# Second mixer's attention with the values stationary and the turned probabilities moving; GpSimd normalises before the turning

## Chip, cores and metric

One core of a Trainium2 chip runs one program: a hybrid layer (neighbourhood attention beside a state-space scan, then a gated feed-forward), and behind it a layer of windowed attention with its own feed-forward. The metric is the device time in microseconds. The kernel before takes 1371.63 us, the median of three runs (1370.94 to 1371.93).

## What is computed

The change lies in the mixer of the second layer: 512 tokens in four blocks of 128, 16 query heads over 4 key and value heads of 64 features. A block sees itself and its two neighbours, and each head has one sink logit that takes a part of the softmax and carries no value.

```python
def windowed_gqa_sink(h, w_qkv, w_o, sink, rel_bias):
    q, k, v = split(h @ w_qkv)                  # 1024, 256 and 256 columns
    scores = einsum('bnqhgd,bnkhd->bnhgqk', q, k_band) * (dh ** -0.5)
    logits = where(mask, scores + bias, -1e30)  # k_band: blocks n-1, n, n+1
    p = softmax(concatenate([logits, sink_l], -1), -1)[..., :-1]
    out = einsum('bnhgqk,bnkhd->bnqhgd', p, v_band)
    return out.reshape(B, S, ATT_Q_HEADS * dh) @ w_o
```

So a head has four blocks of queries, with 2, 3, 3 and 2 blocks of keys: ten blocks of 128 by 128 probabilities.

## The kernel before

**Numbers in two parts.** Products are taken to nearly full precision: a float32 operand is split into a high part that is rounded to the faster type fp32r and a low part, the rest; ScalarE writes the high part (a copy), VectorE the low one (a subtraction). A projection is then three matmuls (`mm3`, L88 to L91: high by high, low by high, high by low). A matmul whose operands are plain float32 is not split by the kernel; it appears in the profile as two weight loads and two matmuls.

**Stages.** First layer's mixer, its feed-forward, the second layer's attention (about 815 to 1000 us of the profile), and its feed-forward. `wide` (L943) makes a projection 128 columns at a time: for each such tile the weights come by DMA from a fixed list (`load_w`, L134: ScalarE L151, VectorE L152), 24 matmuls of 512 columns fill a bank of PSUM (L89 to L91), and `use` takes it from there. Attention is hung on `use` (`use_and_attend`, L1094): after two tiles of keys and one of queries the values are made (L1099 to L1109), and from then on each further tile of queries is followed by two heads; the last two heads follow the last tile.

**A head** (`head`, L1044). For each of the four query blocks: two matmuls make the scores (L1059, L1060; 256 or 384 columns); VectorE adds the bias and finds the row's maximum in one instruction (L1062); ScalarE takes the exponential and its sum (L1064); TensorE turns the 2 or 3 blocks (`tr`, L1067; a transpose is a matmul with the identity); ScalarE or VectorE in turn copies the turned blocks to SBUF (L1072, L1070); and for each block the turned probabilities are loaded as weights while the 64 value columns move (L1075, plain float32, ten per head, 320 matmuls in the profile for 16 heads). Then the sum with the sink is formed and inverted (L1076 to L1078), and one VectorE instruction scales the result by it into the natural layout `on` (L1079). After heads 13 and 15, `turn_o` (L1084) turns one half of `on` each (heads 0 to 7, heads 8 to 15) back to features by tokens (L1088, 32 transposes in all) and splits it (L1090, L1091) for the output projection `att_w_o` (`nat_out`, L826; its matmuls are L836).

**What sets the order.** The code above is written head after head, but a scheduler of the framework lays out each engine's instructions when the program is built, with estimates of its own; it mixes the matmuls of the next query tile between the steps of the heads. On the chip each engine then runs its list strictly in that order. Buffers are rings: three banks for scores, two for turned blocks, one for the heads' output, two for projections.

Of the kernel before, what the change touches and what calls it, by code (L numbers as in the profile page):

```python
# [38 lines left out]
def tile_hybrid_then_windowed_gqa(ctx, tc, A, out, dbg=None):  # L39
# [15 lines left out]
    def H():  # L55
        """h^T in two parts, 8 blocks of features each, tokens along"""
        return [hp_.tile([128, 8, S], F32R, tag=t, name=nm(t)) for t in ("hh", "hl")]
# [8 lines left out]
    def psum(**roles):  # L66
        """the eight banks, shared out anew"""
        for r, ids in roles.items():
            ring = itertools.cycle(ids)
            pst[r] = lambda ring=ring: banks[next(ring)]()  # L70
# [31 lines left out]
    def chunks():  # L102
        """every piece of a weight, in the order of its use: tensor, row block, row blocks, columns"""
# [30 lines left out]
    def load_w(src, k0, nk, pieces, room=None):  # L134
        """the next piece of the plan as two fp32r parts, in halves of a row if room is given;
        the pieces after it are on their way"""
# [34 lines left out]
    # ada_w columns of the first shift and scale, 128 features each at a time  # L171
# [45 lines left out]
    def gemv(src, c0, ci):  # L217
        """partial sums, over the partitions, of vec @ src[:, c0:c0 + 1024]; in steps, the last gives the sums"""
# [35 lines left out]
    def mod_job(o, src, c_sh, c_sc, ci, b_sh, b_sc, w, bank):  # L254
        """o: columns of shift, and of norm weight * (1 + scale); in steps, which leave the engines free between"""
# [6 lines left out]
    def gate_job(g, src, c0, ci, rb, rw, bank):  # L262
        """g: gate as a row on all partitions, times a norm weight if there is one; in steps"""
# [27 lines left out]
    # vec @ ada_w for c and c_ctx at once: rows c hi, c_ctx hi, c lo, c_ctx lo, which pick2 then adds  # L291
# [55 lines left out]
    def features(rows, j, v, hi, lo, n):  # L347
        """features 128 j.. of the modulated rows, features on partitions"""
# [49 lines left out]
    def wide_tile(W, c0, hh, hl, n=S, w=None):  # L398
        """PSUM tile [W columns c0..c0 + 127, n tokens]"""
# [34 lines left out]
    # rows 0..15 hi @ h, rows 16..31 lo @ hi of h; pick16 adds the two  # L434
# [12 lines left out]
    p = PT()  # L447
# [67 lines left out]
    # cum[i] - cum[j] on [j, (head of four, i)] is a product: left [group; -cum[j] of the group], right [cum[i]; 1]; cum in two parts  # L515
# [303 lines left out]
    def tick(n):  # L819
        """n steps of about a microsecond went to the tensor engine: what was put off till then"""  # L820
# [5 lines left out]
    def nat_out(src, lhs, evac, ks, after=None, room=None, roomy=2):  # L826
        """[tokens, 1024] = lhs @ src over row blocks ks; the last few go a token block at a time,
        roomy of them with their weights in tiles of room"""
# [54 lines left out]
    def to_hT(mod, row=None):  # L883
        """h^T and what fills it with a token block; with a row, of the norm with that weight, which settle leaves in x"""
# [58 lines left out]
    def wide(W, hh, hl, cols, use):  # L943
        """tiles of (W column block)^T h^T; the first four run a half of the tokens at a time"""
# [67 lines left out]
    PP = slots(ap_, "pp", 3)  # L1012

# [7 lines left out]
    on = [ap_.tile([128, 4, 512], F32, tag=f"on{a}", name=f"on{a}") for a in range(2)]  # L1021
# [20 lines left out]
    po2 = []  # L1042

    def head(h):  # L1044
        kvh = h // 4
        bt = BI(n=384)
        nc.sync.dma_start(out=bt, in_=A["bias2"][h])
        if h % 2 == 0:
            po2.append(PO())
# [223 lines left out]
```

## Time and profile before

| what | value |
|---|---|
| median of three runs | 1371.63 us |
| span of the profiled execution (the page gives no other time of it) | 1369.5 us |
| busy, whole span | TensorE 97%, VectorE 58%, ScalarE 44%, GpSimd 7% |
| granted TensorE clock, mean | 0.991 of full speed |
| stretch 835 to 960 us | the heads: TensorE 124.2 us busy of 125, GpSimd idle |

How to read it: the span runs from the first to the last instruction; a timed run also holds what lies around it. PE is TensorE's matmuls, PEld its weight loads, DVE VectorE, ACT ScalarE, POOL GpSimd. Matmuls are pipelined, so the duration of one (some 270 ns for a small one) is longer than the distance from one start to the next; what a matmul costs the engine is read from starts, or from the chain of waits, which gives each stretch of time to one instruction only.

### The profile page before, as it was taken

How to read it: one execution, taken by the hardware profiler on the slowest of the kernel's cores; microseconds unless marked ns; L12 is line 12 of the kernel's file. 1: busy time of each engine (PE TensorE's matmuls, PEld its weight loads, DVE VectorE, ACT ScalarE, POOL GpSimd, SP SyncE). 2: the span in 40 equal slices, each digit the busy share in tenths (PEclk: the TensorE clock that was granted, in tenths of full speed). 3: DMA queues.
4: the chain of work that ended last, by engine and by line, in shares of the span. 5: the costliest groups of instructions: out<-in, count | busy, mean ns of one | idle time of the engine just before them, and what ended most of it. 6: DMA issues, size and time to landing. Idle time of an engine off the chain costs nothing. (4 is left out here: it accounts for less than half of the span.)

```text
span 1369.5 us, 18243 instructions
## 1 busy us (share of the span) xinstructions
PE 1332.8 (97%) x6943; PEld 1108.9 (81%) x6943; DVE 793.5 (58%) x1432; ACT 599.5 (44%) x1076; POOL 95.5 (7%) x101
## 2 busy tenths in 40 slices
PE   7999999999999999999999989999999999999997
PEld 3688778887879888888888789888888888888886
DVE  4887985447567747765963566666463222225323
ACT  4656446654626333333432456656462222224321
POOL 0012650000000000000000220000000000000000
PEclk9999999999999999999999999999999999999999
DMA  9955111025192637764764303211223333332221
GB/s 287 266 183 153 34 54 51 24 84 182 34 312 86 186 104 232 232 199 138 245 220 135 93 16 101 76 61 43 78 78 94 106 93 93 102 98 93 95 90 62
DMA packets 176631, 168.15 MB, mean 123 GB/s; under 512 B 7584, under 2 KB 153120, under 8 KB 176544
## 3 DMA queue, kind: packets, MB, share of 16 engines
q1 hardware_dynamic: 176544, 166.99, 38.9%
q8 instruction: 55, 0.90, 0.3%
q14 instruction: 32, 0.26, 0.1%
HBM read 164.87 MB, written 2.10 MB: 122 GB/s over the span
## 5 line engine op out<-in xcount | busy, mean ns | idle before, releaser
L90 PE MATMUL bank<-hl,wh 128*128 128x512 f32 (+1 forms) x1040 | 388.4, 373 | 1.3 <-DVE hl L928 0.7
L91 PE MATMUL bank<-hh,wl 128*128 128x512 f32 (+1 forms) x1040 | 388.1, 373 | 0.0
L89 PE MATMUL bank<-hh,wh 128*128 128x512 f32 (+1 forms) x1040 | 387.9, 375 | 0.0
L151 ACT ACTIVATE wh<-wr 128x1024 fp32r<-128x1024 f32 x173 | 182.4, 1059 | 413.1 <-PE bank L90 302.0
L152 DVE TENSOR_TENSOR wl<-wr,wh 128x1024 fp32r<-128x1024 f32 x173 | 213.8, 1237 | 204.1 <-ACT wh L151 204.0
L90 PEld LDWEIGHTS bank<-hl,wh 128*128 128x128 f32 x1040 | 196.7, 189 | 32.3 <-DVE hl L928 1.7
L89 PEld LDWEIGHTS bank<-hh,wh 128*128 128x128 f32 x1040 | 196.2, 189 | 32.7 <-DVE hh L927 0.6
L91 PEld LDWEIGHTS bank<-hh,wl 128*128 128x128 f32 x1040 | 196.8, 189 | 31.8
L836 PE MATMUL bank<-wh,act 128*128 128x512 f32 x544 | 146.2, 389 | 0.0
L836 PEld LDWEIGHTS bank<-wh,act 128*128 128x128 f32 x544 | 102.1, 188 | 21.5 <-issue 0.2
L226 DVE SCALAR_TENSOR_TENSOR acc<-ada,cs,acc 128x1024 f32<-128x1024 f32 x70 | 91.5, 1308 | 16.0 <-DMA ada<-in_ada_w 15.4
L836 PE MATMUL bank<-wl,act 128*128 128x512 f32 x272 | 84.1, 389 | 0.0
L983 DVE TENSOR_TENSOR act<-bank,act 128x512 f32<-128x512 f32 x44 | 30.4, 690 | 89.7 <-PE bank L91 89.6
L207 POOL TENSOR_TENSOR sm<-sm,mh 128x1 f32<-128x1 f32 x28 | 18.3, 654 | 660.3 <-DVE sm L206 660.3
L836 PEld LDWEIGHTS bank<-wl,act 128*128 128x128 f32 x272 | 51.0, 188 | 10.6
L836 PE MATMUL bank<-act,act 128*128 128x512 f32 x240 | 55.2, 390 | 0.0
L836 PEld LDWEIGHTS bank<-act,act 128*128 128x128 f32 x240 | 44.9, 188 | 9.2
L1075 PEld LDWEIGHTS bank<-v,pp 128*128 128x128 f32 x320 | 41.3, 191 | 5.5 <-ACT pp L1072 2.3
L1075 PE MATMUL bank<-v,pp 128*128 128x64 f32 x320 | 43.1, 271 | 0.1
L993 DVE TENSOR_TENSOR act<-act,act 128x512 fp32r<-128x512 f32 x44 | 29.4, 686 | 21.9 <-PE bank L836 21.9
L1064 ACT ACTIVATE sc<-sc,ss 128x256 f32<-128x256 f32 (+1 forms) x64 | 35.6, 557 | 12.7 <-DVE ss L1062 8.8
L1062 DVE CUSTOM_DVE_ANT_0 sc<-bank,bi,nsink 128x256 f32<-128x256 f32 (+1 forms) x64 | 33.6, 542 | 10.1 <-PE bank L1060 8.2
(333 smaller groups left out, 1946.6 us busy)
## 6 DMA issues: line engine op xcount, KB each, us to landing
ada<-in_ada_w SPq DMA_DIRECT2D x80, 512.0 KB, 4.9
wr<-in_ffn_w_up SPq DMA_DIRECT2D x44, 512.0 KB, 4.5
wr<-in_ffn_w_in SPq DMA_DIRECT2D x44, 512.0 KB, 3.7
wr<-in_w_in SPq DMA_DIRECT2D x23, 512.0 KB, 3.9
wr<-in_ffn_w_down SPq DMA_DIRECT2D x22, 512.0 KB, 4.3
wr<-in_ffn_w_out SPq DMA_DIRECT2D x22, 512.0 KB, 3.5
wr<-in_att_w_qkv SPq DMA_DIRECT2D x12, 512.0 KB, 3.9
ada<-in_ada_w SPq DMA_DIRECT2D x16, 256.0 KB, 4.8
```

Of the source, the lines that this page charges most:

```text
L89: mm(o, lh, rh, start=start, stop=False)
L90: mm(o, lh, rl, start=False, stop=False)
L91: mm(o, ll, rh, start=False, stop=stop)
L151: act(hi[:, :n], raw[:, :n], AF.Copy)
L152: V.tensor_sub(lo[:, :n], raw[:, :n], hi[:, :n])
L226: V.scalar_tensor_tensor(acc, raw, csil[:, ci + k:ci + k + 1], acc, op0=ALU.mult, op1=ALU.add)
L836: mm(ps[tb][a], l, r[a], start=start and l is lh and r is w[0], stop=stop and l is ll)
L983: V.tensor_mul(actT[ft], p, actT[ft])
L993: V.tensor_sub(lo, actT[k], hi)
L1062: V.tensor_tensor_reduce(sc[:, :w], s[:, :w], bt[:, b0:b0 + w], -1.0, nsink[:, h:h + 1], ALU.add, ALU.min, st[:, n:n + 1])
L1064: act(sc[:, :w], sc[:, :w], AF.Exp, scale=-1.0, bias=st[:, n:n + 1], accum_out=st[:, 4 + n:5 + n])
L1075: mm(o, P[:, 128 * i:128 * i + 128], vv[j0 + i][:, 64 * kvh:64 * kvh + 64], start=i == 0, stop=i == nk - 1)
```

## The change

The head is cut in two. The four softmaxes come first and leave four blocks of exponentials in seven buffers (`sc_ring`: four of the ring `xn`, three of `sc`); then the sum with the sink is formed and inverted. In the second half GpSimd multiplies each block of exponentials by the row's inverse sum (L1072 of the changed kernel), TensorE turns them as before (L1075), ScalarE writes the high part of the turned probabilities (L1079) and VectorE the low part (L1080) into two tiles `ph` and `pl`, one of each for the whole kernel, laid out by key block. The values stand in two parts side by side, 64 columns high and 64 low, and are loaded as the 128 weight columns; for each of the four key blocks the 256 or 384 turned columns that see it move past them, first high, then low (L1086: eight matmuls a head, all in fp32r). The result has features on partitions: the products with the high values in one half of the partitions, with the low values in the other. ScalarE copies one half across (L1092), VectorE adds the other (L1093), and after each second head the pair is split once (L1096, L1097) and is ready as one row block of the output projection. `turn_o`, the copies L1070 and L1072 and the scaling L1079 of the kernel before are gone.

```diff
-    PP = slots(ap_, "pp", 3)
+    sc_ring = itertools.cycle([XN] * 4 + [PS_] * 3)
...
-            sc = PS_(n=384)
+            sc = next(sc_ring)(n=384)
             V.tensor_tensor_reduce(sc[:, :w], s[:, :w], bt[:, b0:b0 + w], -1.0, nsink[:, h:h + 1],
                                    ALU.add, ALU.min, st[:, n:n + 1])
             act(sc[:, :w], sc[:, :w], AF.Exp, scale=-1.0, bias=st[:, n:n + 1], accum_out=st[:, 4 + n:5 + n])
+            scs.append(sc)
+        act(st[:, 8:12], st[:, 0:4], AF.Exp, bias=sk[:, h:h + 1])
+        V.tensor_add(st[:, 12:16], st[:, 4:8], st[:, 8:12])
+        V.reciprocal(st[:, 16:20], st[:, 12:16])
+
+        ph, pl = (ap_.tile([128, 4, 512], F32R, tag=f"on{a}", name=nm("p")).rearrange("p a b -> p (a b)")
+                  for a in range(2))
+        for n, (j0, j1) in enumerate(spans):
+            nk, sc = j1 - j0, scs[n]
+            GP.tensor_scalar(sc[:, :128 * nk], sc[:, :128 * nk], st[:, 16 + n:17 + n], None, op0=ALU.mult)
             pt = PT()
             for i in range(nk):
                 tr(pt[:, 128 * i:128 * i + 128], sc[:, 128 * i:128 * i + 128], ident)
-            P = PP(n=384)
-            if n % 2:
-                V.tensor_copy(P[:, :w], pt[:, :w])
-            else:
-                act(P[:, :w], pt[:, :w], AF.Copy)
-            o = po[:, 64 * n:64 * n + 64]
-            for i in range(nk):
-                mm(o, P[:, 128 * i:128 * i + 128], vv[j0 + i][:, 64 * kvh:64 * kvh + 64], start=i == 0, stop=i == nk - 1)
...
-        V.tensor_tensor(on[h // 8][:, :, 64 * (h % 8):64 * (h % 8) + 64], hd(po, 4),
-                        st[:, 16:20, None].to_broadcast([128, 4, 64]), op=ALU.mult)
+            at = 256 * j0 + 128 * n + 128
+            hi, lo = (t[:, at:at + 256 * nk].rearrange("p (k n) -> p k n", k=nk)[:, :, 0:128] for t in (ph, pl))
+            src = pt[:, :128 * nk].rearrange("p (k n) -> p k n", k=nk)
+            act(hi, src, AF.Copy)
+            V.tensor_sub(lo, src, hi)
+        po = PO()
+        for j in range(4):
+            n0, n1 = max(0, j - 1), min(4, j + 2)
+            a = 384 * j + 128 * (n0 - j + 1)
+            for part in (ph, pl):
+                mm(po[:, 128 * n0:128 * n1], vv[j][:, 128 * kvh:128 * kvh + 128], part[:, a:a + 128 * (n1 - n0)],
+                   start=j == 0 and part is ph, stop=j == 3 and part is pl, skip_group_check=True)
+        own, other = slice(64 * (h % 2), 64 * (h % 2) + 64), slice(64 - 64 * (h % 2), 128 - 64 * (h % 2))
+        if h % 2 == 0:
+            op.append(TM())
+        o = op[-1]
+        act(o[own, :], po[other, :], AF.Copy)
+        V.tensor_add(o[own, :], po[own, :], o[own, :])
+        if h % 2:
+            hi, lo = Q(F32R), Q(F32R)
+            act(hi, o, AF.Copy)
+            V.tensor_sub(lo, o, hi)
+            oT[h // 2] = hi, lo
...
-    def turn_o(a):
-        for tb in range(4):
-            p = PT()
-            for f in range(4):
-                tr(p[:, 128 * f:128 * f + 128], on[a][:, tb, 128 * f:128 * f + 128], ident)
-            hi, lo = Q(F32R), Q(F32R)
-            act(hi, p, AF.Copy)
-            V.tensor_sub(lo, p, hi)
-            oT[tb, a] = hi, lo
...
-                t = VV()
-                V.tensor_copy(t, pv)
-                vv.extend([t[:, 0:256], t[:, 256:512]])
+                t = VV(F32R, 1024)
+                tv = t.rearrange("p (g s d) -> p g s d", g=8, s=2)
+                act(tv[:, :, 0, :], hd(pv, 8), AF.Copy)
+                V.tensor_sub(tv[:, :, 1, :], hd(pv, 8), tv[:, :, 0, :])
+                vv.extend([t[:, 0:512], t[:, 512:1024]])
...
-        hi, lo = oT[tb, k // 4]
-        c = slice(128 * (k % 4), 128 * (k % 4) + 128)
+        hi, lo = oT[k]
+        c = slice(128 * tb, 128 * tb + 128)
         return hi[:, c], lo[:, c]
```

The scheduler lays the new program out anew. Two places show how the instructions stand (L numbers of the kernel concerned; a number behind a name tells one use of a buffer from another).

TensorE, head 6 before, from its second score block to its third turned block: `bank_7779` is the head's output, L1067 the turning, L1075 the product with the values, L89 to L91 the next query tile.

```order
L1067 MATMUL bank_7800<-id_102,sc_7797 128x128 x3
L89 MATMUL bank_7910<-hh_6599,wh_7906 128x512
L1059 MATMUL bank_7872<-q_7065,q_7610 128x384
L1060 MATMUL bank_7872<-q_7068,q_7610 128x384
L90 MATMUL bank_7910<-hl_6600,wh_7906 128x512
L91 MATMUL bank_7910<-hh_6599,wl_7907 128x512
L1075 MATMUL bank_7779<-v_7232,pp_7790 128x64 x2
L1067 MATMUL bank_7815<-id_102,sc_7812 128x128 x3
```

TensorE, head 6 now: `bank_7883` is the head's output, L1075 the turning, L1086 the product with the values (`p_7855` high, `p_7856` low), L1057 the next pair's scores.

```order
L1075 MATMUL bank_7858<-id_102,xn_7831 128x128 x2
L1075 MATMUL bank_7864<-id_102,sc_7837 128x128 x3
L90 MATMUL bank_7974<-hl_6600,wh_7970 128x512
L91 MATMUL bank_7974<-hh_6599,wl_7971 128x512
L89 MATMUL bank_7974<-hh_6599,wh_7970 128x512
L1086 MATMUL bank_7883<-p_7855,v_7230 128x256
L90 MATMUL bank_7974<-hl_6600,wh_7970 128x512
L91 MATMUL bank_7974<-hh_6599,wl_7971 128x512
L1075 MATMUL bank_7871<-id_102,sc_7843 128x128 x3
L89 MATMUL bank_7974<-hh_6599,wh_7970 128x512
L1075 MATMUL bank_7878<-id_102,sc_7849 128x128 x2
L1086 MATMUL bank_7883<-p_7856,v_7230 128x256
```

Before, a product followed its own block's turning and copying; now the first product waits for two blocks, the other seven for all or nearly all, and three matmuls of the query tile stand between.

ScalarE, the same pair before: L1064 the exponentials, L1072 the copies of turned blocks, L1076 the sink, L1037 a query tile.

```order
L1064 ACTIVATE sc_7812,ss_7780<-sc_7812,ss_7780 128x384
L1037 ACTIVATE q_7774<-bank_7746 64x512
L1072 ACTIVATE pp_7790<-bank_7787 128x256
L1064 ACTIVATE sc_7827,ss_7780<-sc_7827,ss_7780 128x256
L1076 ACTIVATE ss_7780<-ss_7780,misc_806 128x4
L1072 ACTIVATE pp_7819<-bank_7815 128x384
```

ScalarE, the end of head 6 now: L1079 the high parts of head 6 (`p_7855`), L1062 and L1064 the exponentials and the sink of head 7, L1096 the split of the pair 4 and 5, L1036 a query tile, L1092 the copy across of head 6.

```order
L1079 ACTIVATE p_7855<-bank_7858 128x2x128
L1079 ACTIVATE p_7855<-bank_7864 128x3x128
L1096 ACTIVATE q_7784<-tm_7712 128x512
L1062 ACTIVATE xn_7913,ss_7897<-xn_7913,ss_7897 128x384
L1036 ACTIVATE q_7819<-bank_7794 64x512
L1079 ACTIVATE p_7855<-bank_7871 128x3x128
L1079 ACTIVATE p_7855<-bank_7878 128x2x128
L1062 ACTIVATE xn_7919,ss_7897<-xn_7919,ss_7897 128x256
L1036 ACTIVATE q_7822<-bank_7794 64x512
L1064 ACTIVATE ss_7897<-ss_7897,misc_806 128x4
L151 ACTIVATE wh_8676<-wr_8328 128x1024
L1092 ACTIVATE tm_7892<-bank_7883 64x512
```

All four turned blocks now pass through ScalarE, where two of four did; between the last high part and the copy across stand other work of the neighbouring heads and a weight tile.

## Rows read from the trace of the kernel before

**Rows 1.** The page: span and busy time, whole program.

```profile
span 1369.5 us, 18243 instructions
PE 1332.8 (97%) x6943; PEld 1108.9 (81%) x6943; DVE 793.5 (58%) x1432; ACT 599.5 (44%) x1076; POOL 95.5 (7%) x101
```

**Rows 2.** Busy us by stretch (length, PE, PEld, DVE, ACT, POOL, clock, DMA): heads; four pairs.

```profile
835.00:960.00 125.00, 124.19 (x849) 108.61 (x849) 82.89 (x241) 78.16 (x209) 0.00 (x0) 1.00 0.20 61
...
sum 58.00, PE 58.00 PEld 50.98 DVE 38.60 ACT 36.22 POOL 0.00; mean PE 14.50 PEld 12.75 DVE 9.65 ACT 9.06 POOL 0.00
```

**Rows 3.** Instructions in time, ScalarE: the same copy in two query tiles that follow.

```profile
883.21 0.57 ACT L1037 ACTIVATE q<-bank 64x512 fp32r<-64x512 f32 x1
...
898.03 0.58 ACT L1037 ACTIVATE q<-bank 64x512 fp32r<-64x512 f32 x1
```

**Rows 4.** The chain of waits, 850 to 925 us, shares by line.

```profile
by line: PE bank L1075 30.1%; PE bank L1067 15.1%; PE bank L90 13.1%; PE bank L91 12.7%; PE bank L89 12.3%; PE bank L1059 9.2%; PE bank L1060 7.8%
```

**Rows 5.** Instructions in time, TensorE: start and length of runs.

```profile
903.13 1.45 PE L1075 MATMUL bank<-v,pp 128*128 128x64 f32 x12
904.41 0.39 PE L1067 MATMUL bank<-id,sc 128*128 128x128 f32 x2
```

**Rows 6.** Groups by form, 835 to 960 us, ScalarE.

```profile
L1064 ACT ACTIVATE sc<-sc,ss 128x384 f32<-128x384 f32 x32 | 19.5, 610 | 2.4 <-DVE ss L1062 2.4
...
L1072 ACT ACTIVATE pp<-bank 128x384 f32<-128x384 f32 x16 | 7.9, 492 | 4.2 <-PE bank L1067 3.9
L1037 ACT ACTIVATE q<-bank 64x512 fp32r<-64x512 f32 x12 | 7.0, 584 | 0.1
L1072 ACT ACTIVATE pp<-bank 128x256 f32<-128x256 f32 x16 | 6.1, 384 | 4.2 <-PE bank L1067 4.1
L1090 ACT ACTIVATE q<-bank 128x512 fp32r<-128x512 f32 x8 | 4.7, 596 | 5.3 <-PE bank L1088 5.3
```

**Rows 7.** Groups by form, 850 to 925 us, VectorE.

```profile
L1038 DVE SCALAR_TENSOR_TENSOR q<-bank,q 64x512 fp32r<-64x512 f32 x10 | 6.9, 688 | 0.3
L152 DVE TENSOR_TENSOR wl<-wr,wh 128x1024 fp32r<-128x1024 f32 x5 | 6.1, 1220 | 0.0
L1070 DVE COPY pp<-bank 128x384 f32<-128x384 f32 x10 | 5.6, 558 | 0.2
L1070 DVE COPY pp<-bank 128x256 f32<-128x256 f32 x11 | 4.7, 425 | 13.7 <-ACT ss L1076 9.5 <-PE bank L1067 4.1
L1079 DVE TENSOR_TENSOR on<-bank,ss 128x256 f32<-128x256 f32 x10 | 4.2, 425 | 4.9 <-PE bank L1075 4.9
```

**Rows 8.** Instructions in time, VectorE: two that follow each other at once.

```profile
883.12 0.61 DVE L1062 CUSTOM_DVE_ANT_0 sc<-bank,bi,nsink 128x384 f32<-128x384 f32 x1
...
883.66 0.61 DVE L1062 CUSTOM_DVE_ANT_0 sc<-bank,bi,nsink 128x384 f32<-128x384 f32 x1
```

**Rows 9.** Groups by form, GpSimd, whole program.

```profile
L622 POOL TENSOR_TENSOR sp<-tri,dtv 128x512 f32<-128x512 f32 x16 | 20.3, 1273 | 75.5 <-DVE dtv L469 60.3 <-DVE sc L628 14.6
...
L600 POOL TENSOR_TENSOR t<-n,wend 128x256 f32<-128x256 f32 x12 | 9.0, 778 | 5.3 <-ACT n L585 5.3
...
masks.py:199 POOL TENSOR_SCALAR_AFFINE_SELECT id<-id 128x128 f32<-128x128 f32 x1 | 0.3, 292 | 0.1
```

**Rows 10.** Busy time, 130 to 200 us: the first mixer's scan (columns as Rows 2).

```profile
130.00:200.00 70.00, 63.71 (x338) 50.09 (x336) 63.78 (x96) 34.88 (x62) 46.35 (x45) 1.00 0.19 56
```

**Rows 11.** Groups by form, VectorE, 130 to 200 us.

```profile
L152 DVE TENSOR_TENSOR wl<-wr,wh 128x1024 fp32r<-128x1024 f32 x4 | 7.0, 1738 | 0.0
...
L645 DVE TENSOR_TENSOR t<-bank,ex 128x512 f32<-128x512 f32 x8 | 5.4, 681 | 0.5 <-PE bank L643 0.5
```

**Rows 12.** Instructions in time, VectorE and GpSimd: one operation beside GpSimd, then alone.

```profile
796.57 1.27 POOL L902 TENSOR_TENSOR xn<-x,ada 128x512 f32<-128x512 f32 x1
...
796.83 2.10 DVE L932 SCALAR_TENSOR_TENSOR x<-x,rx,ada 128x1024 f32<-128x1024 f32 x1
...
803.50 1.28 DVE L932 SCALAR_TENSOR_TENSOR x<-x,rx,ada 128x1024 f32<-128x1024 f32 x1
```

More of the change, by code (lines that the diff above doesn't have):

```diff
@@ L1020, in tile_hybrid_then_windowed_gqa @@
     V.tensor_scalar(nsink, sk, -1.0, None, op0=ALU.mult)
-    on = [ap_.tile([128, 4, 512], F32, tag=f"on{a}", name=f"on{a}") for a in range(2)]
     vv = []
@@ L1040, in use_qkv @@
                 qs[2 * (i - 2) + s] = t
-    po2 = []
+    op = []
     def head(h):
@@ L1047, in head @@
         nc.sync.dma_start(out=bt, in_=A["bias2"][h])
-        if h % 2 == 0:
-            po2.append(PO())
-        po, st = po2[-1][:, 256 * (h % 2):256 * (h % 2) + 256], SS(n=20)
-        for n in range(4):
-            j0, j1 = max(0, n - 1), min(4, n + 2)
-            nk = j1 - j0
-            w = 128 * nk
+        st, scs = SS(n=20), []
+        spans = [(max(0, n - 1), min(4, n + 2)) for n in range(4)]
+        for n, (j0, j1) in enumerate(spans):
+            w = 128 * (j1 - j0)
             b0 = 128 * (j0 - n + 1)
@@ L1064, in head @@
             act(sc[:, :w], sc[:, :w], AF.Exp, scale=-1.0, bias=st[:, n:n + 1], accum_out=st[:, 4 + n:5 + n])
+            scs.append(sc)
[4 more added lines that the diff above has]
+                  for a in range(2))
+        for n, (j0, j1) in enumerate(spans):
+            nk, sc = j1 - j0, scs[n]
+            GP.tensor_scalar(sc[:, :128 * nk], sc[:, :128 * nk], st[:, 16 + n:17 + n], None, op0=ALU.mult)
             pt = PT()
@@ L1067, in head @@
                 tr(pt[:, 128 * i:128 * i + 128], sc[:, 128 * i:128 * i + 128], ident)
-            P = PP(n=384)
-            if n % 2:
-                V.tensor_copy(P[:, :w], pt[:, :w])
-            else:
-                act(P[:, :w], pt[:, :w], AF.Copy)
-            o = po[:, 64 * n:64 * n + 64]
-            for i in range(nk):
-                mm(o, P[:, 128 * i:128 * i + 128], vv[j0 + i][:, 64 * kvh:64 * kvh + 64], start=i == 0, stop=i == nk - 1)
-        act(st[:, 8:12], st[:, 0:4], AF.Exp, bias=sk[:, h:h + 1])
-        V.tensor_add(st[:, 12:16], st[:, 4:8], st[:, 8:12])
-        V.reciprocal(st[:, 16:20], st[:, 12:16])
-        V.tensor_tensor(on[h // 8][:, :, 64 * (h % 8):64 * (h % 8) + 64], hd(po, 4),
-                        st[:, 16:20, None].to_broadcast([128, 4, 64]), op=ALU.mult)
-    oT = {}
-    def turn_o(a):
-        for tb in range(4):
-            p = PT()
-            for f in range(4):
-                tr(p[:, 128 * f:128 * f + 128], on[a][:, tb, 128 * f:128 * f + 128], ident)
-            hi, lo = Q(F32R), Q(F32R)
-            act(hi, p, AF.Copy)
-            V.tensor_sub(lo, p, hi)
-            oT[tb, a] = hi, lo
+            at = 256 * j0 + 128 * n + 128
[21 more added lines that the diff above has]
+            oT[h // 2] = hi, lo
+    oT = {}
     def use_and_attend(i, p):
@@ L1113, in use_and_attend @@
                 head(h)
-        if i == 9:
-            turn_o(0)
     wide(Wq, hh, hl, qkv_cols, use_and_attend)
@@ L1119, in tile_hybrid_then_windowed_gqa @@
         head(h)
-    turn_o(1)
     def lhs_o(tb, k):
-        hi, lo = oT[tb, k // 4]
-        c = slice(128 * (k % 4), 128 * (k % 4) + 128)
+        hi, lo = oT[k]
+        c = slice(128 * tb, 128 * tb + 128)
         return hi[:, c], lo[:, c]
```

## Prediction
> **What bounds it now.** I read the busy times first, then the stretch of the heads, then the chain of waits there, then groups by shape for the prices, and last a stretch of the first mixer, the only one in which GpSimd works hard beside the others. Over the program TensorE is busy 97%, and in the 125 us of the heads 124.2 [rows 1, 2]; VectorE has 82.9 and ScalarE 78.2 there, and GpSimd nothing. So the heads are bound by TensorE, and the two others have a third of the time free. The work repeats with each query tile, which brings two heads (a pair): the same copy starts 14.82 us apart [rows 3], and there are eight pairs. The chain of waits over 75 us, which is 5.06 pairs, is TensorE alone and says what each kind of matmul costs [rows 4]: the products with the values (L1075) 30.1%, 4.46 us a pair; the scores (L1059, L1060) 17.0%, 2.52; the turning (L1067) 15.1%, 2.24; the query tile (L89 to L91) 38.1%, 5.65. Starts agree: twelve product matmuls take 1.28 us, 0.107 each [rows 5], and a pair has 40.
>
> **TensorE after.** A pair has 16 products in place of 40. They have the columns (eight of 256, eight of 384), the type and the full weight load of the 16 score matmuls, so I price them as those: 2.52 us. A pair falls to 14.82 - 4.46 + 2.52 = 12.88 us, 1.94 less, 15.5 for eight. The 32 transposes of `turn_o` (twice four tiles of four) go; at 2.24 us for 20 one costs 0.112, so 3.6 us. TensorE gets 19.1 us shorter. Turning and tiles stay.
>
> **ScalarE after.** Its 9.06 us in 14.5 [rows 2] are 9.26 in a pair. Four copies of turned blocks become eight high parts of the same two shapes: minus 1.75, plus 3.50 (0.492 and 0.384 each, [rows 6]). Two copies across (as L1037, 0.584) add 1.17, the split of the pair (as L1090) 0.60. Sum 12.8.
>
> **VectorE after.** 9.65 in 14.5 are 9.86. Gone are four copies (1.97) and two scalings (0.85); new are eight low parts (two operands from PSUM and SBUF cost what the copy costs, 0.425 at 256 columns for both, [rows 7]; 3.93), two additions (as L1038, 0.688; 1.38) and the low part of the pair (0.69). Sum 13.0. That is an upper figure: instructions that follow each other at once overlap, 0.54 from start to start where each lasts 0.61 [rows 8], so some 30 in a pair can give back 2 us, and 11 is the lower one.
>
> **GpSimd, new.** The trace has no multiplication by a column there. Bounds: two-input operations take 0.778 us at 256 columns and 1.273 at 512, so 1.03 at 384 between them; the one-input operation takes 0.292 at 128 columns, and a larger one can't be quicker [rows 9]. I take 0.78 and 1.03, the rows of its size: 7.2 us a pair, half of the time, so GpSimd itself is no bound. The blocks are normalised in a latency of a few us that the seven buffers let run ahead of the turning; the turning waits for it, and behind a turning that waits stands all of TensorE's list, the query tile too. The Trainium skill (GPSIMD Engine Reference, section 4.1 Engine selection) has one-input elementwise work at roughly line rate there; by that the eight operations would take an estimated 2 us a pair and the clash with VectorE in the next part would shrink by two thirds; the forecast would be about 1360 us. No row here shows this operation.
>
> **GpSimd beside VectorE.** In the scan, where GpSimd is busy 66% [rows 10], the weight split with both inputs in SBUF takes 1.738 us in place of 1.220, while one with an input in PSUM keeps its 0.681 [rows 7, 11]. In a pair the two large operations with both inputs in SBUF are that split (plus 0.52) and the pair's low part (plus 0.29 by the same ratio); at half the time in place of two thirds, 0.6 us. VectorE: 13.7 upper, 11.7 lower. The low parts read PSUM and are spared.
>
> **The pair's length.** Three in-order engines at 12.9, 12.8 and 11.7 to 13.7 us can't all be full. The scan is the nearest stretch, with GpSimd in its chain: TensorE and VectorE were each busy 91% there [rows 10]. TensorE by that: 12.88/0.91 = 14.15. The ends are 12.9 (nothing waits) and 13.7/0.91 = 15.05 (VectorE binds without overlap). I take 14.1, 0.7 us less than now, 5.6 for eight pairs.
>
> **What costs nothing.** The values' split (two ScalarE and two VectorE instructions more, once) runs beside the query tiles that were laid ahead. After the last head a copy, an addition and the split (about 2.6 us) come before the last row block of the output projection; seven other row blocks are ready by then, since pairs and no longer eight heads make a row block, and the first four are laid out between the last heads. If those run out, the 2.6 us show. No DMA is added; on SP's queue a few loads of output weights change places with a head's bias, where the DMA engines are 20% busy [rows 2].
>
> **The sum.** 5.6 + 3.6 = 9.2 us. On the profiled execution that is 1369.5 - 9.2 = 1360.3 of span; the median of the runs stands 2.1 above the span (1371.63), so **1362.4 us**. With pairs of 13.4 to 14.6 us the forecast's own range is 1356.6 to 1366.3.
>
> **Rivals.**
> *TensorE stays the bound.* The layout fits, nothing waits: 19.1 us gained, 1352.5. For it: TensorE waited 0.8 us in 125 before. Against: three engines at the same load. 0.10.
>
> *The copies eat it.* VectorE binds at 15.05 us a pair: plus 1.8, minus 3.6, so 1369.8, which is no change. For it: 13 us of VectorE's work without a gap. Against: the overlap. 0.15.
>
> *The port between GpSimd and VectorE* (slower). The one clash in rows: an operation of 1.28 us took 2.10 when GpSimd had started 0.26 us before it and had 1.01 us to go [rows 12]; it lost 0.82, most of the rest of GpSimd's operation. In a pair four VectorE operations have both inputs in SBUF (the weight split, the pair's low part, two sums of four columns), and eight GpSimd operations follow each other closely. If each of the four waits out a whole 1.03 us, VectorE needs 13.0 + 4.1 = 17.1 us: plus 18.2 for eight pairs, minus 3.6, so 1386. It makes the kernel slower from 15.3 us a pair on (14.82 and an eighth of 3.6), that is if a wait costs over 0.55 us on average. Against: GpSimd is idle half of the time, and the scan's splits lost 0.52 at two thirds. The Trainium skill (SBUF — State Buffer, section Who interferes with whom) says that such a pair shares a read interface under a lock, held for the whole instruction, and the second blocks fully; the clash above agrees to 0.2 us. 0.10.
>
> *One set of probability tiles* (slower). `ph` and `pl` exist once: the next head's first high part on ScalarE waits until the last product has read them, and behind it wait the exponentials. After the last high part come a low part (0.56), seven products (1.1), two tile matmuls (0.47) and four scores (0.63) in order: 2.8 us. ScalarE's list has there four exponentials, two copies, the sink and a weight tile; the two larger exponentials (0.610 each) and the copies (0.584 each) alone are 2.4 us [rows 6], so it should be covered. If half of it isn't, a pair takes 12.8 + 2.8 = 15.6 us plus waits, say 16.0: plus 9.4, minus 3.6, 1377.4. 0.10.
>
> **Numbers.** Forecast 0.55, rivals 0.10, 0.15, 0.10, 0.10. The range runs from the TensorE bound to the last rival, 1352.5 to 1378, and leaves out the port's full price and the tails. About 0.2% (2.7 us) is what can be told from no change here. Faster is forecast and TensorE bound, 0.65; same the copies, 0.15; slower the last two, 0.20.
>
> **What would show it.** Right: eight pairs of about 14.1 us; product matmuls 0.118 and 0.173 from start to start like the scores; TensorE busy about 91 to 95% of the heads' stretch, with small waits of turnings on GpSimd and of products on the low parts; VectorE near 90%; L1080 at 0.43 and 0.56 us, and weight splits that lengthen. The chain of waits should lose its pure TensorE look there. Wrong: GpSimd operations well over 1.03 us or with queues before them (the port), ScalarE idle before its first high part until products end (the tiles), TensorE full (its bound), or a pair that is no shorter with VectorE over 95%. A granted TensorE clock below 1.00 in the heads would be a cost I have not priced.

## The result and the profile after

The changed kernel takes 1381.47 us (median of eleven runs, 1376.37 to 1388.45) against 1371.96 of the kernel before in the same sessions (1370.6 to 1379.47). The ratio is 1.0058, with a 95% interval of 1.0038 to 1.0079. That is slower by more than the 0.2% that can be told here; the forecast was 1362.4, and its range ended at 1378. In the sessions of the experiments below the kernel before took 1372.6 to 1373.2 us; differences between two experiments are differences of their medians.

The profiled execution of the changed kernel took 1380.78 us, 1379.0 of it span, so the two executions differ by 9.5 us of span, as the medians do. The page answers to [rows 1]:

```profile
span 1379.0 us, 17979 instructions
...
PE 1325.5 (96%) x6719; PEld 1093.6 (79%) x6719; DVE 812.1 (59%) x1464; ACT 619.4 (45%) x1126; POOL 167.6 (12%) x165
```

TensorE is busy 7.3 us less and ends 9.5 us later. In both executions the second mixer's key tiles are copied from 828 us of the profile on; the last matmul of its output projection starts at 996.6 us before and at 1006.2 now. So all of the loss lies between. By stretch, with the same columns as [rows 2], the heads of the changed kernel are:

```profile
850.00:870.00 20.00, 17.23 (x98) 14.12 (x97) 15.53 (x44) 14.51 (x40) 12.42 (x11) 1.00 0.15 47
870.00:890.00 20.00, 16.59 (x85) 13.62 (x84) 13.81 (x36) 13.56 (x36) 9.91 (x9) 0.91 0.21 62
...
910.00:930.00 20.00, 16.54 (x90) 12.51 (x89) 15.47 (x44) 15.57 (x43) 12.14 (x12) 1.00 0.10 29
930.00:950.00 20.00, 17.30 (x88) 13.47 (x87) 16.00 (x41) 14.24 (x39) 10.05 (x9) 0.90 0.22 71
950.00:970.00 20.00, 18.91 (x101) 15.65 (x101) 12.89 (x38) 12.34 (x34) 12.83 (x12) 0.93 0.02 8
sum 135.00, PE 117.02 PEld 93.56 DVE 97.18 ACT 94.37 POOL 72.44; mean PE 16.72 PEld 13.37 DVE 13.88 ACT 13.48 POOL 10.35
```

In [rows 2] TensorE was busy 124.2 us of 125 at a clock of 1.00. Now, in 835 to 970 us, 18 of 135 us are idle, and the clock is below 1.00 in three of these stretches. The stretches before the first two of them have TensorE busy for 17.23 and 16.54 of 20 us. These figures are means of two levels, 1.00 (2.4 GHz) and 0.50 (1.2 GHz), as narrower windows show: TensorE was busy about half of 4 us, and then ran at the lower level.

```profile
942.00:946.00 4.00, 2.04 (x11) 0.98 (x9) 2.53 (x8) 2.66 (x7) 4.00 (x4) 1.00 0.18 49
946.00:948.00 2.00, 1.65 (x6) 1.23 (x6) 1.97 (x3) 2.00 (x8) 0.24 (x1) 0.50 0.03 9
```

No engine is full: in 835 to 970 us VectorE works 72% and ScalarE 70% of the time, GpSimd 54%. So it isn't a new bound by load; it is waiting. Two query tiles that lie four pairs apart give the pair's length (instructions in time, ScalarE, the copy that answers to [rows 3]):

```profile
862.32 0.58 ACT L1036 ACTIVATE q<-bank 64x512 fp32r<-64x512 f32 x1
...
931.07 0.57 ACT L1036 ACTIVATE q<-bank 64x512 fp32r<-64x512 f32 x1
```

That is 68.75 us for four, 17.2 a pair on average (15.3 to 18.8), where it was 14.82. Who waits is seen best from the side of the new step. The view of one line, L1072, in 835 to 970 us, gives GpSimd's durations (shortest, median, longest in ns) and who waited for it (us, times):

```profile
L1072 POOL TENSOR_SCALAR xn<-xn,ss x37: 922/1242/2256, 844.8 to 966.7; 128x256 f32<-128x256 f32 x19, 128x384 f32<-128x384 f32 x18
L1072 POOL TENSOR_SCALAR sc<-sc,ss x27: 921/1242/1831, 850.2 to 965.5; 128x384 f32<-128x384 f32 x14, 128x256 f32<-128x256 f32 x13
...
who waited for it (us, times):
  PEld bank L1075: 26.7, 34
  PE bank L1075: 16.7, 27
```

TensorE's matmuls stood 16.7 us for GpSimd (its weight loads, which could have run further ahead, 26.7): nearly all of the 18 idle us. One head shows how. Instructions in time, 902.3 to 907.9 us (start, length, engine, line, in brackets the idle time before and who ended it):

```profile
902.44 0.16 DVE L1066 RECIPROCAL ss<-ss 128x4 f32<-128x4 f32 x1
...
902.79 5.60 POOL L1072 TENSOR_SCALAR xn<-xn,ss 128x256 f32<-128x256 f32 x4 [5.09 <-DVE ss L1066]
...
903.04 1.21 DVE L152 TENSOR_TENSOR wl<-wr,wh 128x1024 fp32r<-128x1024 f32 x1
903.05 0.39 PE L89 MATMUL bank<-hh,wh 128*128 128x512 f32 x1
...
905.10 0.44 PE L1075 MATMUL bank<-id,xn 128*128 128x128 f32 x2 [1.66 <-POOL xn L1072]
905.63 0.38 ACT L1079 ACTIVATE p<-bank 128x256 fp32r<-128x256 f32 x1 [1.78 <-PE bank L1075]
906.05 0.42 DVE L1080 TENSOR_TENSOR p<-bank,p 128x256 fp32r<-128x256 f32 x1 [1.80 <-ACT p L1079]
906.32 0.55 PE L1075 MATMUL bank<-id,xn 128*128 128x128 f32 x3 [0.78 <-POOL xn L1072]
906.62 0.42 PE L1057 MATMUL bank<-q,q 128*128 128x384 f32 x1
```

The inverse sum is there at 902.60. GpSimd, idle for 5.09 us until then, starts 0.19 us later, and four multiplications take 5.60 us. Between the sum and the first turning TensorE's list holds too little: its last matmul of the query tile starts at 903.05, then it stands 1.66 us. After two transposes it stands 0.78 us more for the second block, and only behind that come the next scores (L1057), which need nothing from GpSimd. ScalarE and VectorE wait in a row for the same cause. Here VectorE's weight split (903.04, two inputs in SBUF) kept its 1.21 us, while GpSimd took longer: the first turning starts 2.31 us after GpSimd's start, where an undisturbed multiplication of that size takes 0.92.

### The profile page after: what moved, and what is told of

The parts are those of the page before. It is cut to its first block, busy times and chain, and to the rows that moved or that the text cites. A ratio compares the mean times of both kernels' runs of the same rounds, so it can differ in the third digit from the quotient of the medians.

```text
span 1379.0 us, 17979 instructions
## 1 busy us (share of the span) xinstructions
PE 1325.5 (96%) x6719; PEld 1093.6 (79%) x6719; DVE 812.1 (59%) x1464; ACT 619.4 (45%) x1126; POOL 167.6 (12%) x165
## 5 line engine op out<-in xcount | busy, mean ns | idle before, releaser
L91 PE MATMUL bank<-hh,wl 128*128 128x512 f32 (+1 forms) x1040 | 387.7, 373 | 0.0
L89 PE MATMUL bank<-hh,wh 128*128 128x512 f32 (+1 forms) x1040 | 387.6, 375 | 0.0
L89 PEld LDWEIGHTS bank<-hh,wh 128*128 128x128 f32 x1040 | 196.5, 189 | 32.8 <-DVE hh L927 0.5
L91 PEld LDWEIGHTS bank<-hh,wl 128*128 128x128 f32 x1040 | 197.0, 189 | 31.7
L902 POOL TENSOR_TENSOR xn<-x,ada 128x512 f32<-128x512 f32 x8 | 10.6, 1320 | 353.3 <-DVE x L876 347.0
L1072 POOL TENSOR_SCALAR xn<-xn,ss 128x256 f32<-128x256 f32 (+1 forms) x37 | 43.0, 1175 | 66.4 <-DVE ss L1066 50.5
L1080 DVE TENSOR_TENSOR p<-bank,p 128x256 fp32r<-128x256 f32 (+1 forms) x64 | 30.3, 487 | 18.8 <-ACT p L1079 17.3
L923 ACT ACTIVATE tm<-bank,mod 128x128 f32<-128x128 f32 x96 | 36.0, 460 | 7.0 <-PE bank L920 6.9
```

Of the source, the lines that this page charges most:

```text
L89: mm(o, lh, rh, start=start, stop=False)
L91: mm(o, ll, rh, start=False, stop=stop)
L923: act(full[:, 128 * i:128 * i + 128], p[:, 128 * i:128 * i + 128], AF.Identity, scale=mod[:, 8 + k:9 + k], bias=mod[:, k:k + 1])
L1072: GP.tensor_scalar(sc[:, :128 * nk], sc[:, :128 * nk], st[:, 16 + n:17 + n], None, op0=ALU.mult)
L1080: V.tensor_sub(lo, src, hi)
```

## The experiments

Three theories were put up first. **G**: GpSimd's multiplication stands in front of TensorE's in-order list and is dearer than priced. **T**: the one set of probability tiles holds ScalarE up. **C**: the added copies on ScalarE and VectorE are the bound. Then G was split: does the multiplication cost because TensorE waits for it (latency), or because GpSimd's work disturbs VectorE (port)? The pair's length below is taken as above, from the first copies of query tiles that lie four or five pairs apart.

### Without the multiplication

```diff
-            GP.tensor_scalar(sc[:, :128 * nk], sc[:, :128 * nk], st[:, 16 + n:17 + n], None, op0=ALU.mult)
```

> The changed kernel without the 64 multiplications on GpSimd: the probabilities stay unnormalised, all else is the same (part left out: the division by the softmax sum). Theory G (GpSimd's multiplication stands in front of TensorE's in-order list and is dearer than priced, 0.92 and 1.24 us alone, up to 2.26 beside a weight split): the turnings wait no more, 1358 to 1366 us, pairs of 14.0 to 14.5 us, granted clock 1.00 in the heads. Theory T (one set of probability tiles): 1376 to 1382, ScalarE waits for the products. Theory C (the added copies on ScalarE and VectorE): 1372 to 1380.

Measured: 1358.66 us, ratio to the kernel before 0.9888 [0.9843, 0.9934]. The windows over four pairs, 855.66 to 908.51 us, with the columns of [rows 2]:

```profile
855.66:908.51 52.85, 52.61 (x311) 45.11 (x310) 48.67 (x141) 47.43 (x135) 0.00 (x0) 1.00 0.19 61
```

The time is at the fast end of what theory G expected, and a pair takes 13.2 us, less than the 14.0 to 14.5 written down; TensorE is busy 13.15 of them and the clock is 1.00. T and C keep all their work in this kernel and cost next to nothing: VectorE has 12.2 us and ScalarE 11.9 in a pair, beside a full TensorE. The one line on GpSimd costs 22.8 us (1381.47 less 1358.66). A variant that hides this line wholly should come to about this time.

### Two sets of probability tiles

```diff
-        ph, pl = (ap_.tile([128, 4, 512], F32R, tag=f"on{a}", name=nm("p")).rearrange("p a b -> p (a b)")
-                  for a in range(2))
+        ph, pl = (ap_.tile([128, 1280], F32R, tag=f"on{2 * (h % 2) + a}", name=nm("p")) for a in range(2))
```

The tiles are packed to ten blocks each, and three buffers of the exponentials come from another ring to make room.

> The changed kernel with two sets of probability tiles, packed to ten blocks each; three score buffers move to an idle ring to make room. Theory T: 1368 to 1374, the waits of ScalarE's high parts on products go and the pairs fall to 15 us or less. Theories G and C: 1378 to 1384, no change beyond 3 us, since ScalarE waited only 1.6 us for products in the whole stretch.

Measured: 1389.62 us, ratio 1.0108 [1.0073, 1.0142]. Waits in 835 to 970 us:

```profile
PEld bank L1074 <- POOL xn L1071: 21.1, 22, 2.1
...
PE bank L1074 <- POOL xn L1071: 14.0, 21, 1.7
PEld bank L1074 <- POOL xt L1071: 9.3, 11, 2.1
...
PE bank L1074 <- POOL xt L1071: 6.0, 10, 1.8
```

TensorE's matmuls wait 20.0 us for GpSimd where they waited 16.7. Room for a second head's probabilities gave nothing, so T falls as the main cost. The time is also 5.6 us above the range that G and C expected; why this kernel is slower than the changed one is open (its lists have another order).

### The multiplication on VectorE

```diff
-            GP.tensor_scalar(sc[:, :128 * nk], sc[:, :128 * nk], st[:, 16 + n:17 + n], None, op0=ALU.mult)
+            V.tensor_scalar(sc[:, :128 * nk], sc[:, :128 * nk], st[:, 16 + n:17 + n], None, op0=ALU.mult)
```

> The changed kernel with the multiplication on VectorE in place of GpSimd. A row of before has 0.48 us for 512 columns of such an operation, so about 0.27 and 0.37, 2.6 us a pair. Theory G: the latency goes, VectorE gets 15.6 us a pair at most, 1364 to 1372. Theory C (VectorE's and ScalarE's load binds): slower than the changed kernel, 1384 or more. Theory T: as the changed kernel, 1380.

Measured: 1372.61 us, ratio 1.0001 [0.9981, 1.002], the time of the kernel before and just above theory G's range. Groups by form, VectorE, 835 to 970 us (busy us and mean ns behind the bar):

```profile
L1072 DVE TENSOR_SCALAR xn<-xn,ss 128x384 f32<-128x384 f32 x18 | 7.0, 412 | 0.0
L1072 DVE TENSOR_SCALAR xn<-xn,ss 128x256 f32<-128x256 f32 x19 | 6.6, 347 | 0.2
```

The window over five pairs, columns of [rows 2]:

```profile
859.59:940.43 80.84, 70.56 (x375) 56.45 (x373) 74.59 (x216) 59.80 (x163) 0.00 (x0) 0.96 0.18 58
```

The same instruction takes 0.35 and 0.41 us here, 0.92 and 1.24 on GpSimd. But VectorE now has 14.9 us of work in a pair of 16.2, 92%, and in 835 to 970 us TensorE's matmuls wait 7.7 us for it and 2.9 for ScalarE. So the copies' rival is close here; that VectorE's load alone sets the time is not shown, and the next run speaks against it.

### The same, with GpSimd taking weight splits off VectorE

```diff
-        V.tensor_sub(lo[:, :n], raw[:, :n], hi[:, :n])
+        lowp[0].tensor_sub(lo[:, :n], raw[:, :n], hi[:, :n])
```

`lowp[0]` is GpSimd while the heads run and VectorE elsewhere; the multiplication stays on VectorE.

> As the run with the multiplication on VectorE, and GpSimd makes the low parts of the weight tiles of this stretch in VectorE's place (some 2.3 to 2.6 us each, off the path, since a weight tile is ready long before its use). VectorE loses 1.22 us a pair. Theory G with VectorE as the next bound: 2 to 8 us faster than the run without this, 1360 to 1368. Theory C: no less than 1376.

Measured: 1377.49 us, ratio 1.0031 [1.0013, 1.0048]: slower than without, where 1360 to 1368 was expected. In 835 to 970 us VectorE falls from 119.1 to 114.2 us, yet TensorE is busy 123.6 us where it was 124.1, at a clock of 0.95. Four splits went to GpSimd, at 2.40 us each in place of 1.21, and none of TensorE's waits ends on them; they still end on VectorE (3.9 us on the second half of a query tile, 2.5 on low parts, 2.1 on a normalised block). So 5 us less of work on the fullest engine moved nothing. Why the whole got slower is open.

### GpSimd works, and nobody waits for it

The exponentials are turned as they are, and GpSimd writes its products into a tile of their own (normalisation is left out of the result).

```diff
-            GP.tensor_scalar(sc[:, :128 * nk], sc[:, :128 * nk], st[:, 16 + n:17 + n], None, op0=ALU.mult)
+            GP.tensor_scalar(XT(n=384)[:, :128 * nk], sc[:, :128 * nk], st[:, 16 + n:17 + n], None, op0=ALU.mult)
```

> The changed kernel with the turning reading the exponentials as they are; GpSimd still does its 64 multiplications by the inverse sum, of the same sizes and at the same places, but into a tile that nothing reads (the result is left without the normalisation). So GpSimd has its full work beside VectorE, and TensorE does not wait for it. Theory latency (the multiplication costs because TensorE's list stands behind it): as fast as without the multiplication, 1357 to 1363 us, pairs of 13.1 to 13.5 us, clock 1.00 in the heads. Theory port (GpSimd's work slows VectorE down, wherever its result goes): at least half of the 22.8 us stays, 1370 us or more, with weight splits near 2 us on VectorE and pairs of 15 us. A time of 1364 to 1369 would put a part on each.

Measured: 1357.68 us, ratio 0.9883 [0.9839, 0.9927], the time of the kernel without the multiplication. The window over four pairs, columns of [rows 2]:

```profile
861.82:914.98 53.16, 52.96 (x311) 44.71 (x310) 49.41 (x142) 47.52 (x136) 39.80 (x35) 1.00 0.20 61
```

The view of line L1072 in 835 to 970 us (durations, and who waited for it):

```profile
L1072 POOL TENSOR_SCALAR xt<-xn,ss x37: 921/1246/1832, 849.0 to 950.3; 128x256 f32<-128x256 f32 x19, 128x384 f32<-128x384 f32 x18
...
who waited for it (us, times):
  DVE xn L1060: 1.4, 2
```

Groups by form in the same stretch, VectorE's weight splits:

```profile
L152 DVE TENSOR_TENSOR wl<-wr,wh 128x1024 fp32r<-128x1024 f32 x12 | 14.6, 1217 | 8.8 <-ACT wh L151 8.8
```

GpSimd is busy 75% of these four pairs (39.80 of 53.16 us), more densely than in the changed kernel (38.32 of 68.75, 56%), and the other engines lose next to nothing by it: the weight splits keep 1.22 us. So the port between GpSimd and VectorE is not what costs. The wait is.

### More buffers, the same order

```diff
-    sc_ring = itertools.cycle([XN] * 4 + [PS_] * 3)
+    sc_ring = itertools.cycle([XN] * 4 + [PS_] * 3 + [XT] * 3)
```

> The changed kernel with ten buffers for exponentials in place of seven, the program otherwise written in the same order; all of the computation is there. Theory order (what counts is which instructions stand in TensorE's list between a head's scores and its turnings): more buffers alone change little, 1376 to 1388 us, waits of the turnings on GpSimd still over 35 us in the heads. Theory buffers (seven were too few for the scores to run ahead, as three more of them were part of the interleaved run): most of the 22 us comes back, under 1367 us.

Measured: 1377.99 us, ratio 1.0028 [1.0007, 1.0049]. Who waited for the multiplication in 835 to 970 us:

```profile
  PEld bank L1075: 25.2, 35
  PE bank L1075: 14.8, 27
```

TensorE's matmuls still wait 14.8 us for GpSimd and its loads 25.2, where it was 16.7 and 26.7. (The 35 that were expected count both, which overlap.) Ten buffers in place of seven bring 3.5 us of 22.8 at most, since the intervals of the two ratios overlap: the buffers allow a distance between a head's halves, they do not make it.

### The next head's first half ahead of this head's second half

`head` is cut at the inverse sum into `first` (scores, exponentials, sum) and `second` (normalising, turning, products), with the ten buffers of the run above; GpSimd's line is unchanged.

```diff
+    pend = []
+
+    def head(h):
+        pend.append(first(h))
+        if h:
+            second(*pend.pop(0))
...
+    second(*pend.pop(0))
```

> The changed kernel with the first half of head h+1 (scores, exponentials, sum) written ahead of the second half of head h (normalising, turning, products), and three more buffers for exponentials (ten in place of seven); all of the computation is there. Theory latency: the inverse sum of a head is known a half head, some 3 to 4 us, before its turnings are due, so GpSimd's four operations (4.3 us) are mostly done by then; waits of the turnings on GpSimd fall from about 43 us in the heads to under 15, pairs of 13.3 to 14.2 us, 1360 to 1368 us. Theory port or throughput: nothing is gained by distance, waits only change their place, 1374 us or more. If scores wait for a free buffer in place of GpSimd, pairs stay near 15 us and the time near 1372.

Measured: 1359.34 us, ratio 0.9896 [0.9853, 0.9939]. The window over five pairs, columns of [rows 2]:

```profile
850.03:918.71 68.68, 66.96 (x385) 56.50 (x385) 62.18 (x175) 58.37 (x162) 46.78 (x42) 1.00 0.21 68
```

The view of the multiplication's line (now L1081) in 835 to 970 us:

```profile
L1081 POOL TENSOR_SCALAR sc<-sc,ss x18: 923/1244/1816, 849.1 to 937.5; 128x256 f32<-128x256 f32 x9, 128x384 f32<-128x384 f32 x9
...
who waited for it (us, times):
  PEld bank L1084: 2.5, 4
  PE bank L1084: 1.2, 3
```

GpSimd's multiplications last as long as before, and there are as many; TensorE's wait for them falls from 16.7 to 1.2 us, the clock stays at 1.00, and a pair takes 13.7 us. All of the computation is there, and the time is within 1 us of that of the kernel without the multiplication. **This version is faster than both kernels.**

### The same order with the multiplication on VectorE

> As the run with the halves interleaved, but VectorE does the 64 multiplications. All of the computation is there. VectorE then has 13 us and 3.9 more in a pair, about 16 with overlap: theory latency says that distance can not help an engine that is full, so 1368 to 1374 us as with VectorE's multiplication without the interleaving (1372.6), VectorE over 93% busy in the heads. If it comes under 1366, then that earlier run was bound by waits too and not by VectorE's load.

Measured: 1370.97 us, ratio 0.9993 [0.9969, 1.0016]. The time is the expected one, and distance, which took 22 us off with the multiplication on GpSimd, takes under 2 off here. But VectorE's 120.2 of 135 us are 89% and not the 93% written down, so that a full VectorE is the reason fits and is not shown.

### One more multiplication ahead of each head, in either order

The same line goes into the changed kernel and into the interleaved one; its result is not read.

```diff
+            if n == 0:
+                GP.tensor_scalar(SX(n=256), sc[:, :256], st[:, 16:17], None, op0=ALU.mult)
```

> The changed kernel with one more multiplication of 128x256 on GpSimd (0.92 to 1.1 us), into a tile that nothing reads, ahead of each head's first; all of the computation is there. Theory latency: every head's turnings come about 1.0 us later and TensorE's list stands for it, one to one: 16 heads by 0.7 to 1.0 us, 1392 to 1399 us. If TensorE's other work could fill it, under 1385. GpSimd then works 11 us of a pair of 18, so its load binds nothing.

> The interleaved kernel with the same added multiplication on GpSimd ahead of each head's first; all of the computation is there. Theory latency: the distance of a half head has room for it, so at most 4 us more than the interleaved kernel, 1358 to 1364 us, although GpSimd now works some 11 us of a pair of 13.6. If GpSimd's load or its clash with VectorE were what counts, the same 16 us as in the run without the interleaving would be added: 1370 us or more.

Measured: 1403.56 us, ratio 1.0224 [1.0188, 1.026], in the changed kernel's order, and 1365.89 us, 0.995 [0.9931, 0.9968], in the interleaved one. The window over four pairs of the first:

```profile
865.73:946.42 80.69, 64.21 (x305) 51.54 (x304) 50.92 (x140) 48.48 (x130) 46.39 (x42) 0.87 0.15 47
```

The window over five pairs of the second:

```profile
857.15:929.04 71.89, 67.58 (x386) 57.47 (x386) 61.60 (x173) 58.38 (x162) 55.48 (x51) 0.99 0.21 65
```

An instruction of 0.93 us (the median) that nobody reads costs 22.1 us, 1.38 a head, in the first order: more than one to one, and more than expected. The added standing alone is less. Waits of TensorE's matmuls for GpSimd, 835 to 1030 us of the first:

```profile
PE bank L1078 <- POOL xn L1075: 18.8, 18, 2.7
PE bank L1078 <- POOL sc L1075: 9.9, 10, 1.9
```

That is 28.7 us where it was 16.7, so 0.75 a head. The rest goes with the clock: 0.87 in the four pairs above, where the changed kernel had 0.98. These pairs are 11.9 us longer than its four; 4.8 of that is TensorE idle and 7.1 TensorE busy for longer, and busy time by clock is the same 55.9 us in both (64.21 by 0.87, 57.09 by 0.98). In the second order it costs 6.6 us, 0.41 a head. That is above the 4 us that were expected, since GpSimd now has 11.1 us in a pair of 14.4 and the half head no longer covers all of it (TensorE's matmuls wait 5.5 us for the multiplications in 835 to 990 us). But it is under a third of the price in the other order.

### Normalising after the product

```diff
+        GP.tensor_copy(wides[-1].rearrange("p (n a d) -> p a n d", n=4, a=2)[:, h % 2], rc[:, :, None].to_broadcast([128, 4, 64]))
...
+            pb = PT()
+            for n in range(4):
+                tr(pb[:, 128 * n:128 * n + 128], wides[-1][:, 128 * n:128 * n + 128], ident)
+            V.tensor_mul(o, pb, o)
```

The multiplication in front of the turning is gone; `rc` is a head's inverse sum.

> Unnormalised exponentials are turned and multiplied with the values; GpSimd spreads a head's inverse sums over 64 columns (two operations a pair), TensorE turns that into a tile that has each token's factor along the columns (four transposes a pair), and VectorE multiplies the pair's result by it once, 128x512. All of the computation is there. Theory latency: nothing stands in front of the turnings; beside the run without normalisation TensorE gets 0.45 us a pair (four transposes at 0.112) and VectorE 0.69: pairs of 13.5 to 13.8 us and 1361 to 1366 us, faster than both kernels. Rival: VectorE, at 13.7 us of work in a pair, becomes the bound, or the four transposes wait for GpSimd at a pair's end and stop TensorE's list again: pairs of 14.5 us or more, 1370 us or more.

Measured: 1363.08 us, ratio 0.9927 [0.9905, 0.9949]: in the range that was expected, and faster than both kernels too. TensorE waits for none of GpSimd's work there. The pair measures 14.7 us, longer than expected, which meets the rival's condition on the pair, though not on the time; in that stretch (859.76 to 918.60 us) stand ten more 512-column matmuls than in the run without the multiplication, some 0.6 us a pair at 0.23 each. It is 3.7 us behind the interleaved order, which needs no added work on TensorE.

## Why the prediction was wrong

**TensorE after: right.** Without the wait a pair has 13.15 us of TensorE, against 12.88 from the prices of scores and of what was taken away, and some 0.2 us of it are seven small matmuls that the stretch holds beyond four pairs. So products at the price of scores fit.

**ScalarE and VectorE after: right in size.** 12.8 and 11 to 13.7 us were forecast; the changed kernel has 12.2 and 12.7 in a pair (48.76 and 50.91 us in four). The low parts were as priced: 0.419 and 0.555 us, against 0.425 and 0.558 for the copies of [rows 7].

**GpSimd, new: the step that failed.** It failed twice. The size: I took 0.78 and 1.03 us from [rows 9], and the undisturbed operation takes 0.92 and 1.24, so a pair has 8.6 us in place of 7.2, with the disturbed ones 9.2 (73.5 us in eight pairs). The 0.778 of the row was a two-input operation, and no row said that one input can't be dearer. The Trainium skill (GPSIMD Engine Reference, section 4.1 Engine selection) has one-input work at roughly line rate there; the trace doesn't agree, with 1.24 us against VectorE's own 0.41 for the same instruction. But the size alone would have moved little: the run in which nobody reads GpSimd's products shows that all of its work fits beside the others.

The second failure was the sentence that the blocks are normalised "in a latency of a few us that the seven buffers let run ahead of the turning". I named the danger in the next clause (all of TensorE's list stands behind a turning that waits) and gave it no price. Buffers permit running ahead; whether anything does run ahead is decided by the order of the instructions. In the head shown above GpSimd was idle 5.09 us, then began as soon as the sum was there, and the first turning came before the next scores. Only the time between the inverse sum and the first turning in TensorE's list counts as cover, and I could have read it in the program's order. There it was what TensorE did from 902.60 to 903.44 us, 0.84 us. The price could have been bounded from rows: a head's first multiplication at 0.78 and a second at 1.03 us, sixteen times, is 29 us if nothing covers it. That is above the standing (16.7 us) and near the step's whole price (22.8, the clock included), and it would have turned the sign of the forecast.

**The pair's length: wrong with it.** The 91% of the scan [rows 10] is a share of a stretch with another order; it did not carry over. In the changed kernel TensorE was busy 83% of four pairs (57.09 of 68.75 us), and a pair took 17.2 us in place of 14.1.

**The clock was not priced**, as the last part of the prediction says. In 835 to 970 us it is 0.96, where [rows 2] have 1.00: at 117 busy us some 4.7 us. With the 16.7 us in which the matmuls stood for GpSimd that makes 21.4 us, an estimate. The step costs 22.8 us by the medians and 27.6 between the two profiled executions (spans of 1379.0 and 1351.4 us), so 1 to 6 us are not resolved. In the run with the added delay the clock falls further, to 0.87 in four pairs, and takes more there than the added standing does. What GpSimd's wait costs and what the clock adds were not separated by a run of their own.

**GpSimd beside VectorE: the direction was wrong.** I let VectorE's weight splits lengthen by 0.52 us as in [rows 11]. In the changed kernel they take 1.260 us on average, and 1.217 where nobody waits for GpSimd. What lengthens is GpSimd's operation: five of the 64, each beside a weight split, by 0.52 to 1.34 us. In four of the five the split had started first, as here (instructions in time):

```profile
874.10 1.19 DVE L152 TENSOR_TENSOR wl<-wr,wh 128x1024 fp32r<-128x1024 f32 x1
...
874.38 1.71 POOL L1072 TENSOR_SCALAR xn<-xn,ss 128x256 f32<-128x256 f32 x1 [3.38 <-ACT xn L1062]
```

The Trainium skill (SBUF — State Buffer, section Who interferes with whom) says that one of the two is blocked for the whole instruction of the other and that the order of issue decides which. These four agree in direction, and so does [rows 12], where GpSimd had started first and VectorE lost. The head shown above does not: by the records GpSimd started there 0.25 us before the split, and yet the split ran undisturbed while GpSimd lost 1.3 us, about the split's length. Lost to it in the heads is what the 64 operations took over their undisturbed times, 73.5 less 69 us, so 4 us of GpSimd's time.

**The rivals.** The port, as a price on VectorE, is refuted by the run in which nobody waits for GpSimd, two sets of tiles brought no relief, and the copies come near to binding only when VectorE takes the multiplication as well. A sign that I had listed for the port, GpSimd operations well over 1.03 us, was seen all the same; it does not tell the port from a dearer operation. The rival that happened, a turning that waits for GpSimd in front of everything else, was in my text as a remark and not among the rivals. The end of the stage can be accounted for: the last product starts 16.8 us later than before (970.1 against 953.4 us), but 24 fewer matmuls of the output projection (0.23 us each, 5.5 us) and none of 14 transposes of `turn_o` (0.112 each, 1.6 us) stand behind it, so the projection ends 9.6 us later. The whole gain by `turn_o` (3.6 us forecast) was not tried alone.

## What to carry to other kernels

When a step is put in front of an in-order engine, price its latency against the work that stands in that engine's list between the step's input and its first use, not against the buffers or the step's share of the time; if there is less work than latency, the difference is paid each time. When it is short, write the next item's first half ahead of this item's second half before moving the step to another engine: here that, with three more buffers, turned 0.6% slower into 1.0% faster, at the same operations. To tell latency from load, let the engine do its work into a tile that nobody reads.

## What the runs showed of the hardware that was not expected

The multiplication by a column on GpSimd took 0.92 us at 128x256 and 1.24 us at 128x384 (float32, undisturbed), where VectorE took 0.35 and 0.41 us and ScalarE's exponential of the same blocks 0.50 and 0.61. A copy of a column spread over 128x256 took GpSimd 0.40 us in the run that normalises after the product, less than half of the multiplication; but that copy reads only four columns, so the two are not quite alike.

The granted clock averaged 0.80 in one stretch of 10 us of the changed kernel (940 to 950 us, TensorE busy 7.69) and stood at 1.00 in the heads before, where TensorE was busy 124.2 of 125 us. In the run with one more GpSimd operation a head the lower clock cost TensorE more than the added standing did (7.1 against 4.8 us in four pairs).
